# An encoder layer's gate-up groups: the last products and the first split reordered, and one queue of shared weight buffers

## The chip, the cores and the metric

The kernel runs on one core of one Trainium2 chip. The core has a matrix engine (TensorE, PE in the profile; its weight loads are PEld), a vector engine (VectorE, DVE), a scalar engine (ScalarE, ACT), GpSimd (POOL) and a synchronisation engine (SyncE, SP), which here issues most of the transfers from device memory. Each engine takes its instructions in order, and waits for others by semaphores. PE writes its sums into PSUM, eight banks of 128 x 512 float32. The metric is the device time of one execution in microseconds (us).

## The reference

One layer of an encoder, for 256 tokens of width 2048, in float32:

```python
x = x + 0.5 * post1(SwiGLU_1(pre1(x)))
h = pre_m(x); p = h @ W_in              # gated recurrence and windowed attention
x = x + post_m(concat(y_h, y_a) @ W_out)
x = x + 0.5 * post2(SwiGLU_2(pre2(x)))

def swiglu(x, w_gate_up, w_down):       # 2048 -> 2 x 5632 -> 2048
    gate, up = jnp.split(x @ w_gate_up, 2, axis=-1)
    return (jax.nn.silu(gate) * up) @ w_down
```

The change concerns `x @ w_gate_up` in the two feed-forward layers (FFN). All norms here divide by the root mean square.

## The kernel before

**Numbers in two parts.** PE multiplies in a format with fewer bits than float32. So each operand is split into a high part `h` (cast by ACT, line 176) and a low part `l` (the rest, subtracted by DVE, line 177), and each product is three products on PE: h with h, h with l, l with h (`three`, which issues them at line 441). A split of half a weight buffer, `split_half`, is one cast and one subtraction of 128 x 1024. The `h` and `l` buffers are five each, and one comes free when PE has made the last product that reads it.

**Groups and pairs.** The gate-up projection is made in 11 groups (`NG`) of 512 gate and the 512 matching up columns. A group has a 2 x 2 block of results in four PSUM banks, `c[m][n]`: m is the half of the tokens, n is gate or up. `c[0][0]` is called upper left, `c[0][1]` upper right, `c[1][0]` lower left, `c[1][1]` lower right. The sum runs over the width in eight pairs `u` of 128-row blocks. One pair needs 1 MB of weights, `raw`, with the blocks b11, b12 (first 128 rows; gate, up) and b21, b22, loaded by two transfers of 512 KB (line 152).

A plain pair makes eight block products, so 24 products on PE. A *mixed* pair (u = 2, 4, 5, 6; in group 1 only 2 and 4; none in group 0) makes seven block products, 21 on PE, after Strassen's scheme in a variant. For it, sums of weight blocks are formed in `raw`: `prepare` splits b11 (the `h1` and `l1` buffers) and then lets a GpSimd transfer add b12's and b22's source onto the first half of the buffer (line 901); `splits` does two additions on DVE (lines 915 and 916) and splits three halves, "lower", "upper" and "last". Four of the seven products go to four more PSUM banks, p1, p5, p6 and p7; the other three go to `c` directly. `products` (line 485) has their order: p1, upper left, upper right, p5, p7, p6, lower left.

**The boundary.** At the end of a group `boundary` (line 1101) brings the p banks home: ACT copies p1 (line 1112), DVE adds it to the upper left bank (1113), forms p1 + p6 (1116) and adds p7 (1117), adds this to the lower left bank (1118), and so on for upper right (1121, 1122) and lower right (1124, 1125). Pair 7 is plain and its 24 products come last, bank by bank: upper left and lower left after line 1118, upper right after 1122, lower right after 1125. Between 1113 and 1116 it asks for the first half of the split of the next group's pair 0; the second half comes at its end. Then `units` makes silu (ACT, 1039), the gated product (DVE, 1044), a transpose on PE (1064), and the split result `ht` for the down projection. In groups 2 to 5, two of the early `ht` tiles, 512 KB each, are stored to device memory by SP (`put_away`, line 1027), just after the split of pair 6 has been asked for.

**Order.** From group 1 on the order of every engine is written out (`manual_schedule`, line 1167). One function follows another as listed in `first_pairs`, `pair_ahead` and `boundary`: a pair's splits are asked for while the products of the pair before are still to come. Outside of that region a planner orders the instructions by its own estimates, so what is written last is not always last.

**Weight buffers.** Plain pairs use two buffers of the pool `gated.room`, mixed pairs three of `rawp`. `plan` loads the first five: (1,0) plain, (1,2) mixed, (1,1) plain, (1,4) mixed and (2,2) mixed, written (group, pair). After that each split, when it is done with a buffer, calls `load_next` for the next pair of the same kind. So in a usual group the split of pair 0 is followed by the load of pair 3, that of 1 by 7, that of 2 by 6, and those of 3, 4, 5, 6 and 7 by pairs 0, 2, 4, 5 and 1 of the next group. A load waits on SP until its buffer's last reader is done, and SP takes them in the order written.

Of the kernel before, what the change touches and what calls it, by code (L numbers as in the profile page):

```python
# [11 lines left out]
F32 = mybir.dt.float32  # L12
# [8 lines left out]
P = 128  # L21
# [3 lines left out]
KT = D // P  # L25
# [12 lines left out]
def hymba_layer_kernel(  # L38
# [25 lines left out]
    nc = tc.nc  # L64
# [3 lines left out]
    rawp = ctx.enter_context(tc.tile_pool(name="rawp", bufs=3))  # L68
# [7 lines left out]
    def nm(s):  # L76
        uid[0] += 1
        return f"{s}_{uid[0]}"

    def pa():  # L80
        return psum.tile([P, 512], F32, tag="pa", name=nm("pa"))

    def pb():
        return psum.tile([P, 512], F32, tag="pb", name=nm("pb"))
# [56 lines left out]
    def load(src, between=None, pool=rawp, **kw):  # L141
        raw = pool.tile([P, 2048], F32, tag="raw", name=nm("raw"), **kw)
        if len(src.shape) == 4:

            dst = raw.rearrange("p (a n b) -> p a n b", a=src.shape[1], n=src.shape[2])
            parts = [(dst[:, a], src[:, a]) for a in range(src.shape[1])]
        else:
            parts = [(raw.rearrange("p (a b) -> p a b", a=src.shape[1]), src)]
        for i, (to, of) in enumerate(parts):
            if i and between:  # L150
                between()
            nc.sync.dma_start(to, of)
        return raw
# [61 lines left out]
    last = {}  # L215
# [20 lines left out]
    def take(*a):  # L236
        take_hi(*a)
        take_lo(*a)
# [163 lines left out]
    class Blocks:  # L402
# [4 lines left out]
        ahead = None  # L407
# [74 lines left out]
            last = split_half(raw, 1)  # L482
            self.products(u, first, lower, upper, last)

        def products(self, u, first, lower, upper, last):

            if not self.p:
                self.p = [pa(), pa(), pb(), pb()]
            a, w = self.tiles[u], self.left_sums(u)

            def lhs(k, m):
                return [a[:, k, i, m * P : (m + 1) * P] for i in range(2)]

            def summed(j):
                return [w[:, j, i, :] for i in range(2)]

            def rhs(two, n):
                return [x[:, n * 512 : (n + 1) * 512] for x in two]

            for at, left, right in (  # L500
                (("p", 0), lhs(0, 0), first),
                (("c", 0, 0), lhs(1, 0), rhs(lower, 0)),
                (("c", 0, 1), summed(S4), rhs(lower, 1)),
                (("p", 1), summed(S1), rhs(upper, 0)),
                (("p", 3), summed(S3), rhs(upper, 1)),
                (("p", 2), summed(S2), rhs(last, 1)),
                (("c", 1, 0), lhs(1, 1), rhs(last, 0)),
            ):
                self.three(at, *left, *right)

        def fold(self):
# [331 lines left out]
    NG = DFF // 512  # L843
    NU = DFF // 256
    LATE = 8

    MIXED_IN = (2, 4, 5, 6)
    AWAY = 8
    MIXED = range(0, 20, 2)
    MIXED_EARLY = MIXED[:8]  # L850
# [4 lines left out]
    class Gated(Blocks):  # L855
# [20 lines left out]
        def plan(self):  # L876

            self.here = {g: MIXED_IN if g > 1 else MIXED_IN[:2] for g in range(1, NG)}
            self.kinds = {True: [], False: []}
            for g in range(1, NG):  # L880
                for u in range(KT // 2):
                    self.kinds[u in self.here[g]].append((g, u))
            self.raws, self.firsts, self.split_of = {}, {}, {}
            for mixed in (False, True, False, True, True):
                self.load_next(mixed)

        def load_next(self, mixed):

            if self.kinds[mixed]:
                g, u = self.kinds[mixed].pop(0)  # L890
                kw = {} if mixed else {"pool": self.room, "bufs": 2}
                self.raws[g, u] = load(self.source(u, g), **kw)

        def prepare(self, g, u):

# [12 lines left out]
        def splits(self, g, u):  # L908

            raw = self.raws[g, u]  # L910
            got = self.split_of[g, u] = []
            if (g, u) in self.firsts:
                b11, b12, b21, b22 = (raw[:, i * 512 : (i + 1) * 512] for i in range(4))
                got.append(split_half(raw, 1))
                nc.vector.tensor_tensor(b22, b11, b22, ALU.add)
                nc.vector.tensor_tensor(b21, b22, b21, ALU.add)
                yield
                got.append(split_half(raw, 0))
                yield
                got.append(split_half(raw, 1))  # L920
                self.load_next(True)
            else:
                got.append(split_half(raw, 0))
                yield
                got.append(split_half(raw, 1))
                self.load_next(False)
            yield

        def take(self, g, u):

            got = self.split_of.pop((g, u))
            del self.raws[g, u]
            first = self.firsts.pop((g, u), None)
            if first:
                self.products(u, first, *got)
                return ()
            hs, ls = zip(*got)
            return [
                (lambda k=k, m=m, n=n: self.plain(u, hs, ls, m, n, k))
                for k in range(2)  # L940
                for m in range(2)
                for n in range(2)
            ]
# [27 lines left out]
    def ffn(gated, w_dn, post_gain, again, gain=None, lead=None, aside=None):  # L971

        with ExitStack() as st:
            work = st.enter_context(tc.tile_pool(name=nm("wk"), bufs=1, reuse_waits="tile"))
            late = st.enter_context(tc.tile_pool(name=nm("hl"), bufs=LATE, reuse_waits="tile"))
            early_cm = tc.tile_pool(name=nm("he"), bufs=NU - LATE - AWAY, reuse_waits="tile")
            early = early_cm.__enter__()
# [5 lines left out]
            def room_for(tag):  # L983
                return work.tile([P, 512], F32, tag=tag, name=nm(tag))
# [28 lines left out]
            def sums_in(u):  # L1013
# [3 lines left out]
                ws = sums_of(whole, room_for("s").rearrange("p (j t) -> p j t", j=4))  # L1017
                apart = u == MIXED_IN[1]
                w = (gated.room if apart else work).tile(
# [13 lines left out]
            def units(c, scale):  # L1033
# [34 lines left out]
                for bank in banks:  # L1068
                    g = len(hts)
                    u = bank.rearrange("p (k t) -> p k t", k=2)  # L1070
                    if g in MIXED_EARLY:
                        u = room_for("z").rearrange("p (k t) -> p k t", k=2)
                        nc.scalar.copy(u.rearrange("p k t -> p (k t)"), bank)
                    pool = early if AWAY <= g < NU - LATE else late
                    ht = pool.tile([P, 2, 2, T], F32R, tag="ht", name=nm("ht"))
# [6 lines left out]
            def some(steps, n):  # L1082
                for _ in range(n):
                    next(steps)

            pre_stats()
            last = KT // 2 - 1
            for u in range(gated.pos, KT // 2):
# [4 lines left out]
                for done in {4: (0, 1, 2), 5: (3, 4), 6: (5, 6), 7: (7,)}.get(u, ()):  # L1093
                    even(done)
                    if done in MIXED_IN[:2]:
                        sums_in(done)
# [4 lines left out]
            def boundary(g):  # L1101

                a, b = room_for("z"), room_for("s")
                c, (p1, p5, p6, p7) = gated.c, gated.p
                add = nc.vector.tensor_tensor
                rest_of = gated.take(g, last)

                def bank(m, n):
                    for k in range(2):
                        rest_of[4 * k + 2 * m + n]()  # L1110

                nc.scalar.copy(a, p1)
                add(c[0][0], c[0][0], a, ALU.add)  # L1113
                ahead = gated.splits(g + 1, 0)
                next(ahead)
                add(b, p6, a, ALU.add)  # L1116
                add(a, p7, b, ALU.add)  # L1117
                add(c[1][0], c[1][0], a, ALU.add)  # L1118
                bank(0, 0)
                bank(1, 0)  # L1120
                add(b, p5, b, ALU.subtract)
                add(c[0][1], c[0][1], b, ALU.add)
                bank(0, 1)
                add(b, p5, a, ALU.subtract)
                add(c[1][1], c[1][1], b, ALU.add)
                bank(1, 1)
                next(ahead)

            def first_pairs(g, waiting):

                gated.group(g)
                some(waiting, 1)
                gated.prepare(g, MIXED_IN[1])
                some(waiting, 1)
                ahead = gated.splits(g, 1)
                some(ahead, 2)
                gated.prepare(g, MIXED_IN[2])
                for one in gated.take(g, 0):
# [9 lines left out]
            def pair_ahead(g, u):  # L1148

                ahead = gated.splits(g, u + 1)  # L1150
                next(ahead)
                if u + 1 == MIXED_IN[1]:
                    gated.prepare(g, MIXED_IN[3])
# [5 lines left out]
                if g == 1 and u in (4, 5):  # L1159
                    sums_in(MIXED_IN[u - 2])  # L1160
                if u == 5 and 1 < g <= AWAY // 2 + 1:
                    put_away(2 * g - 4)
# [4 lines left out]
            with tc.manual_schedule():  # L1167
                gated.prepare(1, MIXED_IN[0])
                some(gated.splits(1, 0), 2)
                for g in range(1, NG):  # L1170
# [3 lines left out]
                    if g < NG - 1:  # L1174
                        ahead = gated.splits(g, last)
# [24 lines left out]
            close_far()  # L1200
            back_cm = tc.tile_pool(name=nm("hb"), bufs=AWAY, reuse_waits="tile")
            back = back_cm.__enter__()
# [30 lines left out]
    gated = Gated(w_ffn1_gate_up[0], two_banks())  # L1233
    xt = new_xt()
    gated.see(xt)
    with tc.manual_schedule():
# [9 lines left out]
        raw = rawp.tile([P, 2048], F32, tag="raw", name=nm("raw"))  # L1246
        first = gated.source(0)
# [120 lines left out]
    with ExitStack() as s2:  # L1368
# [367 lines left out]
        for hp in range(4):  # L1736
            zf = headpair(2048 + hp * 256, "zf")
            if hp == 1:
                g = gates(0)
# [18 lines left out]
        g = gates(1)  # L1758
# [13 lines left out]
        gated = Gated(w_ffn2_gate_up[0], two_banks())  # L1772
# [80 lines left out]
```

## Time and profile before

| | |
|---|---|
| median of 3 runs | 1850.8 us (1848.57 to 1854.73) |
| the profiled execution | 1851.23 us, span 1849.5 us |
| PE busy | 1816.7 us, 98% |
| DVE busy | 1628.2 us, 88% |
| ACT busy | 1127.2 us, 61% |
| granted clock of PE | 0.999 |

Times in rows count from the start of the span. A row of the timeline gives start, duration, engine, line, operation, output and input tiles, and in brackets how long the engine was idle before it and what released it. Rows of one kind that follow each other are merged (x5). A product's record on PE lasts longer than the distance to the next product, since products overlap. The stretch from 313.49 to 356.37 us is one usual group: 42.88 us. The first FFN's groups 1 to 10 lie between about 57 and 490 us, the second's between about 1181 and 1610 us.

### The profile page before, as it was taken

Reading aid. Unit: us, or ns where it says so; the run is one execution under the profiler, and the core shown is the slowest. Engines: PE = TensorE matmul, PEld = TensorE weight load, DVE = VectorE, ACT = ScalarE, POOL = GpSimd, SP = SyncE. Lnnn points to the kernel's source line nnn. Section 1 sums busy time; section 2 is a strip of 40 time slices with the busy share of each in tenths; the row PEclk is TensorE's granted clock in tenths of the full one; section 3 lists DMA queues with packets and bytes.
Section 4 is the critical chain, followed back from the end, with each engine's and each line's share of the span. In section 5 each row is a group of like instructions: output and inputs, shape, how many; then the busy total and the mean of one; then the engine's idle time right before and its main releaser. Section 6 shows DMA issues by size and latency. Waiting matters only on the chain.

```text
span 1849.5 us, 23264 instructions
## 1 busy us (share of the span) xinstructions
PE 1816.7 (98%) x8438; PEld 1504.2 (81%) x8438; DVE 1628.2 (88%) x2071; ACT 1127.2 (61%) x1492; POOL 114.3 (6%) x115
## 2 busy tenths in 40 slices
PE   9999999999999999999999999999999999999998
PEld 7877878888887888888888888878888778888886
DVE  7999999998999999477687788899999999999897
ACT  7565556655665557477587556555666556666563
POOL 1011111111000000000000000011111111000000
PEclk9999999999999999999999999999999999999999
DMA  8789999888756566656554456789999888865565
GB/s 298 228 219 275 274 268 256 247 244 251 272 186 226 196 248 211 208 175 181 166 171 148 169 212 245 220 237 262 272 272 254 255 246 237 262 236 206 183 237 183
DMA packets 200020, 422.42 MB, mean 228 GB/s; under 512 B 10984, under 2 KB 45888, under 8 KB 199136
## 3 DMA queue, kind: packets, MB, share of 16 engines
q1 hardware_dynamic: 178880, 380.95, 59.9%
q0 software_dynamic: 21024, 39.99, 12.9%
q8 instruction: 66, 1.08, 0.2%
q14 instruction: 50, 0.41, 0.1%
HBM read 408.29 MB, written 12.60 MB: 228 GB/s over the span
## 4 chain that ended last, share of the span: by engine, by line
PE 70%; DVE 14%; DMA 8%; ACT 4%; issue 3%; SPq 1%; POOL 0%; DVEq 0%; ACTq 0%; POOLq 0%
PE pa L441 28%; PE pb L441 25%; DVE l L177 8%; DMA raw<-in_w_ffn_gate_up_dram 6%; PE pa L309 5%; PE pa L314 3%; ACT h L176 3%; PE pa L364 2%; PE pa L363 2%; PE pa L362 2%; DMA raw<-in_w_ffn_down_dram 2%; DVE pb L1118 1%; DVE z L1117 1%; DVE pa L1113 1%; DVE s L1116 1%
## 5 line engine op out<-in xcount | busy, mean ns | idle before, releaser
L176 ACT CAST h<-raw 128x1024 fp32r<-128x1024 f32 (+1 forms) x861 | 846.7, 1013 | 454.2 <-PE pb L441 113.2
L177 DVE TENSOR_TENSOR l<-raw,h 128x1024 fp32r<-128x1024 f32 (+1 forms) x861 | 985.0, 1170 | 136.8 <-ACT h L176 105.5
L441 PE MATMUL pa<-h,xt 128*128 128x512 f32 x1104 | 387.5, 392 | 0.2
L441 PE MATMUL pb<-h,xt 128*128 128x512 f32 x952 | 341.1, 393 | 17.5 <-DVE pb L1118 17.5
L441 PEld LDWEIGHTS pa<-h,xt 128*128 128x128 f32 x1104 | 207.4, 188 | 44.3 <-DVE xt L232 0.6
L441 PEld LDWEIGHTS pb<-h,xt 128*128 128x128 f32 x952 | 178.6, 188 | 64.4 <-DVE pb L1118 25.1
L441 PE MATMUL pa<-l,xt 128*128 128x512 f32 x552 | 215.7, 391 | 0.0
L441 PE MATMUL pb<-l,xt 128*128 128x512 f32 x476 | 185.5, 390 | 0.0
L441 PE MATMUL pb<-h,ht 128*128 128x512 f32 x464 | 163.5, 390 | 0.0
L441 PE MATMUL pa<-h,ht 128*128 128x512 f32 x464 | 162.7, 389 | 0.0
L901 POOL DMA_DIRECT2D raw<-in_w_ffn_gate_up_dram x76 | 92.0, 1211 | 758.1 <-DVE l L177 709.1
L309 PE MATMUL pa<-xt,h 128*128 128x512 f32 x512 | 124.4, 392 | 0.2 <-ACT h L176 0.2
L441 PEld LDWEIGHTS pa<-l,xt 128*128 128x128 f32 x552 | 103.9, 188 | 20.6 <-DVE l L177 0.7
L309 PEld LDWEIGHTS pa<-xt,h 128*128 128x128 f32 x512 | 93.8, 188 | 18.6 <-ACT h L176 0.6
L441 PE MATMUL pa<-h,xs 128*128 128x512 f32 x304 | 105.9, 389 | 0.0
L441 PE MATMUL pb<-h,xs 128*128 128x512 f32 x304 | 105.9, 389 | 0.0
L441 PEld LDWEIGHTS pb<-l,xt 128*128 128x128 f32 x476 | 89.4, 188 | 17.1
L441 PEld LDWEIGHTS pa<-h,ht 128*128 128x128 f32 x464 | 87.1, 188 | 18.2
L441 PEld LDWEIGHTS pb<-h,ht 128*128 128x128 f32 x464 | 87.1, 188 | 18.1
L441 PE MATMUL pb<-l,ht 128*128 128x512 f32 x232 | 90.3, 389 | 0.0
L441 PE MATMUL pa<-l,ht 128*128 128x512 f32 x232 | 90.3, 389 | 0.0
L314 PE MATMUL pa<-xt,l 128*128 128x256 f32 x512 | 69.1, 285 | 0.0
(289 smaller groups left out, 2517.6 us busy)
## 6 DMA issues: line engine op xcount, KB each, us to landing
raw<-in_w_ffn_gate_up_dram SPq DMA_DIRECT2D x350, 512.0 KB, 5.3
raw<-in_w_ffn_down_dram SPq DMA_DIRECT2D x88, 1024.0 KB, 5.2
raw<-in_w_mix_in_dram SPq DMA_DIRECT2D x52, 1024.0 KB, 5.0
raw<-in_w_ffn_gate_up_dram POOLq DMA_DIRECT2D x76, 512.0 KB, 8.3
raw<-in_w_mix_out_dram SPq DMA_DIRECT2D x16, 1024.0 KB, 5.0
away<-ht SPq DMA_DIRECT2D x16, 512.0 KB, 6.6
ht<-away SPq DMA_DIRECT2D x16, 512.0 KB, 7.4
pg<-in_post_norm_ffn_dram SPq DMA_DIRECT2D x4, 512.0 KB, 6.8
```

The source lines that it names most:

```text
L176: nc.scalar.copy(hi, src)
L177: nc.vector.tensor_tensor(lo, src, hi.bitcast(F32), ALU.subtract)
L309: nc.tensor.matmul(slot[f], weights(hs, kk, f), xcol(xt, k), start=(k == 0), stop=(k == KT - 1))
L314: nc.tensor.matmul(slot[f][:, 0:T], weights(ls, kk, f), xcol(xt, kh * 8 + kk, 0), start=False, stop=False,)
L362: nc.tensor.matmul(dst, xh, h[:, o : o + n], start=(k == 0), stop=False)
L363: nc.tensor.matmul(dst, xh, l[:, o : o + n], start=False, stop=False)
L364: nc.tensor.matmul(dst, xl, h[:, o : o + n], start=False, stop=(k == KT - 1))
L441: nc.tensor.matmul(self.bank(at), lhs, rhs, start=(n == 1), stop=n in (ends, self.of[at]), skip_group_check=n > ends,)
L901: nc.gpsimd.dma_start(raw[:, 0:1024].rearrange("p (k c) -> p k c", k=2), self.source(u, g)[:, :, 1], accum_op=ALU.add,)
L1113: add(c[0][0], c[0][0], a, ALU.add)
L1116: add(b, p6, a, ALU.add)
L1117: add(a, p7, b, ALU.add)
```

## The change

Three things are changed, all in the gate-up stage of both FFNs.

- In the last mixed pair (6) of groups 2 to 9 the upper right product comes last. The order is p1, upper left, p5, p7, p6, lower left, upper right. (Group 1 has pair 6 plain; group 10 keeps the old order.)
- In `boundary` the split of the next group's pair 0 is asked for whole, behind all additions and products.
- The five raw buffers are made once and shared by both kinds. Each split that is done with its buffer loads the next pair of one list into it. The list is sorted by when a pair is needed, where a mixed pair counts from its `prepare` (`PREPARED`): in a usual group 2, 0, 4, 1, 5, 3, 6, 7. So the split of pair 0 is followed by the load of pair 3, that of 1 by 6, that of 2 by 7, and those of 3, 4, 5, 6 and 7 by pairs 2, 0, 4, 1 and 5 of the next group. The first five loads are (1,2), (1,0), (1,4) into `rawp` and (1,1), (1,3) into the room.

```diff
-        def products(self, u, first, lower, upper, last):
+        def products(self, u, first, lower, upper, last, order=range(7)):
...
-            for at, left, right in (
+            seven = (
                 (("p", 0), lhs(0, 0), first),
                 (("c", 0, 0), lhs(1, 0), rhs(lower, 0)),
                 (("c", 0, 1), summed(S4), rhs(lower, 1)),
...
-            ):
+            )
+            for i in order:
+                at, left, right = seven[i]
                 self.three(at, *left, *right)
...
+    PREPARED = {2: -0.5, 4: 0.5, 5: 1.5, 6: 3.5}
...
-            self.kinds = {True: [], False: []}
+            wanted = []
             for g in range(1, NG):
                 for u in range(KT // 2):
-                    self.kinds[u in self.here[g]].append((g, u))
+                    before = PREPARED[u] if u in self.here[g] else u
+                    wanted.append((g * KT // 2 + before, g, u))
+            self.wanted = [at[1:] for at in sorted(wanted)]
             self.raws, self.firsts, self.split_of = {}, {}, {}
-            for mixed in (False, True, False, True, True):
-                self.load_next(mixed)
+            for pool, n in ((rawp, 3), (self.room, 2)):
+                for _ in range(n):
+                    raw = pool.tile([P, 2048], F32, tag="raw", name=nm("raw"), bufs=n)
+                    self.load_next(raw)
 
-        def load_next(self, mixed):
+        def load_next(self, raw):
 
-            if self.kinds[mixed]:
-                g, u = self.kinds[mixed].pop(0)
-                kw = {} if mixed else {"pool": self.room, "bufs": 2}
-                self.raws[g, u] = load(self.source(u, g), **kw)
+            if self.wanted:
+                g, u = self.wanted.pop(0)
+                dst = raw.rearrange("p (k n c) -> p k n c", k=2, n=2)
+                for k in range(2):
+                    nc.sync.dma_start(dst[:, k], self.source(u, g)[:, k])
+                self.raws[g, u] = raw
...
-                self.load_next(True)
+                self.load_next(raw)
...
-                self.load_next(False)
+                self.load_next(raw)
...
-                self.products(u, first, *got)
+                before_fold = g < NG - 1 and u == KT // 2 - 2
+                self.products(u, first, *got, (0, 1, 3, 4, 5, 6, 2) if before_fold else range(7))
...
                 add(c[0][0], c[0][0], a, ALU.add)
-                ahead = gated.splits(g + 1, 0)
-                next(ahead)
                 add(b, p6, a, ALU.add)
...
                 bank(1, 1)
-                next(ahead)
+                some(gated.splits(g + 1, 0), 2)
```

## The prediction

> **What bounds the kernel now.** I read the page's first part, the waits of TensorE, the timeline of PE, DVE and ACT around one group boundary, the windows of whole groups, and last the transfers.
>
> ```profile
> span 1849.5 us, 23264 instructions
> PE 1816.7 (98%) x8438; PEld 1504.2 (81%) x8438; DVE 1628.2 (88%) x2071; ACT 1127.2 (61%) x1492; POOL 114.3 (6%) x115
> ...
> PE pb L441 <- DVE pb L1118: 17.5, 18, 1.6
> PE pb L441 <- DVE l L177: 1.5, 2, 0.8
> PE pa L1064 <- DVE s L1044: 0.9, 1, 0.9
> ```
>
> The first line says that PE is the bound nearly everywhere; the list names what its gaps wait for (us, times, longest). Its one large wait is for L1118, the addition into the lower left bank, once at each of the 18 boundaries between gate-up groups (nine in each FFN). How long such a wait is, the starts of the products tell:
>
> ```profile
> 354.93 0.39 PE L441 MATMUL pa<-l,xt 128*128 128x512 f32 x1
> 355.16 0.39 PE L441 MATMUL pa<-h,xt 128*128 128x512 f32 x1
> 356.37 0.50 PE L441 MATMUL pb<-h,xt 128*128 128x512 f32 x1 [0.82 <-DVE pb L1118]
> 356.70 0.40 PE L441 MATMUL pb<-l,xt 128*128 128x512 f32 x1
> ...
> 360.65 0.39 PE L441 MATMUL pa<-h,xt 128*128 128x512 f32 x1
> ...
> 372.60 2.72 PE pa L441 x12
> ```
>
> Undisturbed, twelve products take 2.72, 0.227 each. After 355.16 the next was due at 355.39 and came at 356.37: 0.98 lost, where the idle column says 0.82, because a record lasts 0.39 and hides 0.16. The next group's first product stands at 360.65; from 355.39 it is 18 products away (banks lower left, upper right, lower right), so undisturbed it would come at 355.39 + 18 x 0.227 = 359.47. A usual boundary loses 1.18 in all: 0.98 in the wait and 0.2 in restarts. Over 18 boundaries: 17.5 + 18 x 0.16 = 20.4 of waits, and 18 x 0.2 = 3.6, together 24.0 us that could go. [...]
>
> ```profile
> 347.07 5.38 DVE L177 TENSOR_TENSOR l<-raw,h 128x1024 fp32r<-128x1024 f32 x5
> 352.37 0.69 DVE L1113 TENSOR_TENSOR pa<-pa,z 128x512 f32<-128x512 f32 x1
> 352.97 1.21 DVE L177 TENSOR_TENSOR l<-raw,h 128x1024 fp32r<-128x1024 f32 x1
> 354.10 0.68 DVE L1116 TENSOR_TENSOR s<-pb,z 128x512 f32<-128x512 f32 x1
> 354.82 0.69 DVE L1117 TENSOR_TENSOR z<-pb,s 128x512 f32<-128x512 f32 x1
> 355.61 0.70 DVE L1118 TENSOR_TENSOR pb<-pb,z 128x512 f32<-128x512 f32 x1
> 356.22 0.68 DVE L1121 TENSOR_TENSOR s<-pa,s 128x512 f32<-128x512 f32 x1
> 356.94 0.70 DVE L1122 TENSOR_TENSOR pa<-pa,s 128x512 f32<-128x512 f32 x1
> 357.67 0.69 DVE L1124 TENSOR_TENSOR s<-pa,z 128x512 f32<-128x512 f32 x1
> 358.39 0.70 DVE L1125 TENSOR_TENSOR pb<-pb,s 128x512 f32<-128x512 f32 x1
> 359.00 1.22 DVE L177 TENSOR_TENSOR l<-raw,h 128x1024 fp32r<-128x1024 f32 x1
> 360.13 0.74 DVE L1044 SCALAR_TENSOR_TENSOR z<-pa,scales,z 128x512 f32<-128x512 f32 x1
> ...
> 349.51 1.58 ACT L176 CAST h<-raw 128x1024 fp32r<-128x1024 f32 x2 [0.24 <-ACT h L176]
> 350.99 0.57 ACT L1112 COPY z<-pa 128x512 f32<-128x512 f32 x1
> 351.55 1.05 ACT L176 CAST h<-raw 128x1024 fp32r<-128x1024 f32 x1
> 358.45 0.69 ACT L1039 ACTIVATE z<-pa,scales 128x512 f32<-128x512 f32 x1 [4.54 <-DVE s L1124]
> ```
>
> The first twelve rows are DVE's, the last four ACT's. DVE runs without a gap, and its order is written out: whatever stands ahead of L1118 delays it. Between the first addition (352.37) and L1116 stands the split of the next group's first half (352.97), 1.13 of DVE on the path of L1118.
>
> **The change, part by part.**
>
> *The split goes behind the additions.* I move the rows up, keeping their own distances (0.60 after L1113, then 0.72, 0.79, 0.61, 0.72, 0.73, 0.72): L1116 352.97, L1117 353.69, L1118 354.48 to 355.18, L1122 355.81 to 356.51, L1125 357.26 to 357.96. From L1118's end to PE is 0.06 (356.31 to 356.37). PE wants the lower left bank at 355.39, the upper right at 356.75, the lower right at 358.11; the sums are there at 355.24, 356.57 and 358.02. The wait goes, with margins of 0.15, 0.18 and 0.09.
>
> The two halves of the split follow at 357.87 and 359.00, ending 359.09 and 360.22; L1044 starts at 360.13 as now. The next group's first `l` is wanted at 359.47 + 0.23 = 359.70, the second half's 12 products after 359.47, at 362.2: covers of 0.6 and 2. On ACT, silu waits for L1124, which is over 1.1 earlier.
>
> *The upper right product last.* The group's last mixed pair ends where the six products of the upper left bank begin, at 355.16 - 5 x 0.227 = 354.03; its 21 products began at 349.26. L1116 reads p6. In the old order p6 is products 16 to 18: the last starts at 353.12 and ends at 353.5, too late for 352.97. In the new one it is 13 to 15, ends at 352.8, and fits by 0.15. The upper right bank ends at 354.2, read by L1122 at 355.81: free. So the two edits need each other; with the split alone moved, L1116 would start near 353.6 and PE would still wait 0.4; with the order alone changed, the upper right bank and its buffer come later for nothing. The price: the buffer of the lower half is released at 354.2 instead of 351.5, and ACT's first cast for the next group moves from 351.55 to 354.3; with the second it is done by 356.4, wanted at 357.87.
>
> *Group 1.* Its pair 6 isn't mixed, so only the split moves.
>
> ```profile
> 93.66 0.69 DVE L1113 TENSOR_TENSOR pa<-pa,z 128x512 f32<-128x512 f32 x1
> ...
> 97.66 0.50 PE L441 MATMUL pb<-h,xt 128*128 128x512 f32 x1 [1.34 <-DVE pb L1118]
> ```
>
> L1118 would end 2.81 after L1113's start, at 96.47, PE could go at 96.53, and wants to at 96.17 (97.66 less 1.34 idle and 0.16): 0.36 and 0.2 of restart stay, twice.
>
> *Five shared buffers, in order of need.* The same transfers in the same two pieces of 512 KB, no more instructions on SP or POOL. What triggers them differs: plain pair 1 of the next group now follows the split of pair 6 (was 7); pair 6 that of pair 1 (was 2); mixed pair 5 that of pair 7 (was 6). These matter where `ht` is put away, groups 2 to 5:
>
> ```profile
> 133.81 2.05 SPq L152 DMA_DIRECT2D raw<-in_w_ffn_gate_up_dram  x2
> 135.91 1.07 SPq L1027 DMA_DIRECT2D away<-ht  x2
> 137.08 2.54 SPq L152 DMA_DIRECT2D raw<-in_w_ffn_gate_up_dram  x2
> ...
> 147.72 1.05 ACT L176 CAST h<-raw 128x1024 fp32r<-128x1024 f32 x1 [3.12 <-DMA raw<-in_w_ffn_gate_up_dram]
> 163.80 4.42 ACT L176 CAST h<-raw 128x512 fp32r<-128x512 f32 x5 [3.91 <-DMA raw<-in_w_ffn_gate_up_dram]
> ...
> core 0: us, PE busy (x) PEld busy (x) DVE busy (x) ACT busy (x) POOL busy (x), PEclk, DMA share, GB/s
> ...
> 356.37:399.26 42.89, 42.07 (x188) 34.45 (x189) 39.90 (x48) 26.07 (x30) 4.84 (x4) 1.00 0.87 244
> ...
> 140.58:184.58 44.00, 42.32 (x188) 34.37 (x188) 39.79 (x48) 25.24 (x30) 4.85 (x4) 1.00 0.92 273
> ```
>
> Pair 1's load, issued at 137.08 behind the writes, lands 10.6 later and holds ACT for 3.12; pair 6's holds it for 3.91; that group then takes 44.00. Now pair 1 goes ahead of the writes and pair 6 a pair sooner. Pair 5 takes the place behind the writes, and at 147.7 it is just in time: its first cast follows pair 1's two. The extra waits of such groups are inside the 20.4 above.
>
> *Start of the stage.* The first loads change too: a buffer freed late now takes pair 4 of group 1, where it took one of group 2.
>
> ```profile
> 1176.29 1.20 SPq L152 DMA_DIRECT2D raw<-in_w_ffn_gate_up_dram  x2
> ...
> 54.99 0.62 ACT L176 CAST h<-raw 128x512 fp32r<-128x512 f32 x1 [4.19 <-DMA raw<-in_w_ffn_gate_up_dram]
> ...
> 1180.61 2.01 ACT L176 CAST h<-raw 128x1024 fp32r<-128x1024 f32 x2 [3.23 <-issue]
> ```
>
> Landing 4.1 to 5.3 later (5.3 is the page's median for these), at 1180.4 to 1181.6, its cast (0.53) pushes those at 1180.61, and the silu behind them, by 0.3 to 1.5; PE waits for that silu's product already (L1064, 0.9). The planner, which orders this part, may do better or worse: -0.5 to 2; I take 0.9, the middle. In the first FFN ACT waits for such a load even now, until 54.99, and the list of PE's waits has nothing from it: I take 0.2 of 0 to 1.
>
> At the end of the stage the three buffers that the down projection takes over were last used by pairs 4, 5 and 6 of group 10, and are now by 3, 4 and 5. They come free earlier, and PE waits for no load there: zero.
>
> *The sum.* 24.0, less 0.1 at each of 16 usual boundaries (the margins of 0.09 to 0.18 are thin; bounds 0 and 0.25), 1.6; less 2 x 0.55 for group 1; less 1.1 at the starts: 20.2 gained. The profiled execution took 1851.23 (span 1849.5 and 1.7 around it), 0.4 over the median of 1850.8. From the median: **1830.6**.
>
> **The rivals.**
>
> *Transfers become the bound where `ht` is put away.* For: a DMA share of 0.92 at 273 GB/s in 140.58 to 184.58. Against: 0.92 x 44.00 is 40.5, under the 41.7 that a group would take. If these eight groups keep their period, 8 x 1.18 comes back: 1840. Chance 0.12.
>
> *The bubble stays: DVE can't follow.* PE gains 1.18 a group, DVE has the same work; its casts wait for `h` buffers (0.24 at 349.51). If DVE's slack is spent, L1113 slips after PE by as much, and the wait returns: about 1849. Against: DVE works 39.9 of 42.89 and L1113's start hangs on PE's own release at 349.26, so it comes earlier with PE. [...] Chance 0.05.
>
> *Slower: pair 5's load lands too late.* Behind the writes it heads ACT's queue before pair 2's casts, and all behind wait. In group 3 PE reaches pair 2's first use at about 156.1 (139.6 for the bank, 4.1, then two pairs of 5.44, transposes 0.8, and 0.7); casts and split need 2.8 before, so it may land 16 after its issue without harm. Each us beyond costs 8; 18.7 cancels the gain, at 19.5 it is 1857. Against: 10.6 now. Chance 0.07.
>
> *Thinner margins than read:* 0.4 left at each boundary, 1836 to 1838. Chance 0.08.
>
> **How the numbers follow.** Forecast 0.68, at 1826 to 1835 by its bounds: nothing left at any boundary and the start 0.5 better, against 0.25 left at each and 3 lost at the starts. Adding the thin margins and most of the transfer case gives 1826 to 1841 for eight in ten. A change of 0.3% (5.6 us) is about what a measurement tells from none. Faster: 0.68 + 0.12 + 0.08 = 0.88; same 0.05; slower 0.07.
>
> **What would show it.** L1118 gone from PE's waits except some 0.4 at the two group-1 boundaries; DVE's additions 0.6 to 0.8 apart without L177 among them; usual groups 41.7 to 41.8 long; ACT without its 3.12 and 3.91 waits in groups 2 to 5. Wrong, if a new wait on `l` or on a transfer stands at the boundaries, or a planned part outside them grows.

## The result, and the profile after

| | before | changed |
|---|---|---|
| median | 1852.8 us (1848.57 to 1855.65) | **1831.6 us** (1830.0 to 1832.88) |
| ratio, with its 95% interval | | **0.9887** (0.9864 to 0.991) |
| a second time | 1850.2 us | 1831.8 us, ratio 0.9902 (0.9887 to 0.9917) |
| span of the profiled execution | 1849.5 us | 1831.1 us, the second time 1829.1 us |

The page's first lines for the changed kernel, and rows of PE's waits (us in total, times, longest):

```profile
span 1831.1 us, 23305 instructions
...
PE 1814.2 (99%) x8438; PEld 1504.0 (82%) x8438; DVE 1627.3 (89%) x2071; ACT 1129.4 (62%) x1492; POOL 114.4 (6%) x115
...
PE pb L441 <- DVE l L177: 1.5, 2, 0.8
...
PE pb L441 <- ACT h L176: 1.3, 1, 1.3
PE pa L1074 <- DVE s L1054: 0.9, 1, 0.9
...
PE pb L441 <- DVE pb L1126: 0.4, 2, 0.2
```

The lower left addition (now L1126) has gone from 17.5 us in 18 waits to 0.4 in two, which are those of group 1. New is one wait of 1.3 for a cast; it is outside the groups, and is taken up below. The boundary that answers to the one shown of before, in the timeline (start, duration, engine, line; PE, then DVE, then ACT):

```profile
345.77 0.39 PE L441 MATMUL pa<-h,xs 128*128 128x512 f32 x1
...
347.13 0.39 PE L441 MATMUL pa<-h,xt 128*128 128x512 f32 x1
347.36 0.39 PE L441 MATMUL pb<-h,xt 128*128 128x512 f32 x1
...
351.55 0.39 PE L441 MATMUL pa<-h,xt 128*128 128x512 f32 x1
...
356.99 0.27 PE L1074 MATMUL pa<-ident,z 128*128 128x128 f32 x1
...
344.34 0.69 DVE L1123 TENSOR_TENSOR pa<-pa,z 128x512 f32<-128x512 f32 x1
344.94 0.68 DVE L1124 TENSOR_TENSOR s<-pb,z 128x512 f32<-128x512 f32 x1
345.65 0.69 DVE L1125 TENSOR_TENSOR z<-pb,s 128x512 f32<-128x512 f32 x1
346.45 0.70 DVE L1126 TENSOR_TENSOR pb<-pb,z 128x512 f32<-128x512 f32 x1
347.06 0.68 DVE L1129 TENSOR_TENSOR s<-pa,s 128x512 f32<-128x512 f32 x1
347.84 0.70 DVE L1130 TENSOR_TENSOR pa<-pa,s 128x512 f32<-128x512 f32 x1
348.58 0.69 DVE L1132 TENSOR_TENSOR s<-pa,z 128x512 f32<-128x512 f32 x1
349.30 0.70 DVE L1133 TENSOR_TENSOR pb<-pb,s 128x512 f32<-128x512 f32 x1
349.91 2.35 DVE L177 TENSOR_TENSOR l<-raw,h 128x1024 fp32r<-128x1024 f32 x2
...
344.16 1.05 ACT L176 CAST h<-raw 128x1024 fp32r<-128x1024 f32 x1 [0.62 <-PE pb L441]
345.52 1.06 ACT L176 CAST h<-raw 128x1024 fp32r<-128x1024 f32 x1 [0.30 <-PE pb L441]
```

PE goes from the last product of the upper left bank (347.13) to the first of the lower left (347.36) in 0.23, without a wait: L1126 ended at 347.15. The next group's first product stands at 351.55. The split (L177, 2.35 for both halves) stands behind the last addition. Two windows of the changed kernel (length, then busy time with instructions of PE, PEld, DVE, ACT and POOL, granted clock, DMA share, GB/s), over three of the four groups of a stage where `ht` is put away, and over a usual group:

```profile
core 0: us, PE busy (x) PEld busy (x) DVE busy (x) ACT busy (x) POOL busy (x), PEclk, DMA share, GB/s
104.50:230.00 125.50, 125.50 (x567) 103.53 (x565) 119.58 (x143) 77.92 (x90) 14.72 (x13) 1.00 0.93 275
...
356.99:398.79 41.80, 41.80 (x189) 34.48 (x188) 39.83 (x49) 26.08 (x30) 4.84 (x4) 1.00 0.90 252
```

PE is busy in all of both. By the starts of PE's rows (the transposes after each group, the middle part's first product at line 309, the last product) the execution divides so, in us:

| stretch | before | changed | changed, second time |
|---|---|---|---|
| start to group 0's transposes | 62.6 | 62.5 | 63.3 |
| groups 1 to 10 of the first FFN | 433.0 | 421.8 | 421.8 |
| its down projection and what follows, to line 309 | 291.5 | 293.8 | 290.9 |
| middle part, to the second FFN's group 0 | 399.4 | 399.9 | 400.3 |
| groups 1 to 10 of the second FFN | 433.4 | 423.3 | 423.3 |
| its down projection | 220.5 | 220.9 | 220.6 |

The gain is in the groups: 11.2 and 10.1, together 21.3. Usual groups went from 42.87 to 41.80.

### The profile page after: what moved, and what is told of

Its sections match the earlier page's. It is cut to its first block, busy times and chain, and to the rows that moved or that the text cites. A ratio compares the mean times of both kernels' runs of the same rounds, so it can differ in the third digit from the quotient of the medians.

```text
span 1831.1 us, 23305 instructions
## 1 busy us (share of the span) xinstructions
PE 1814.2 (99%) x8438; PEld 1504.0 (82%) x8438; DVE 1627.3 (89%) x2071; ACT 1129.4 (62%) x1492; POOL 114.4 (6%) x115
## 4 chain that ended last, share of the span: by engine, by line
PE 87%; DVE 5%; ACT 3%; DMA 3%; issue 2%; POOL 0%; SPq 0%; DVEq 0%; ACTq 0%; POOLq 0%
PE pa L441 37%; PE pb L441 33%; PE pa L309 5%; DVE l L177 3%; PE pa L314 3%; DMA raw<-in_w_ffn_gate_up_dram 2%; PE pa L364 2%; PE pa L362 2%; PE pa L363 2%; ACT h L176 1%; PE pa L1074 1%; PE pb L1074 1%; PE pb L1582 0%; PE pb L1556 0%; PE pb L1660 0%
## 5 line engine op out<-in xcount | busy, mean ns | idle before, releaser
L177 DVE TENSOR_TENSOR l<-raw,h 128x1024 fp32r<-128x1024 f32 (+1 forms) x861 | 983.1, 1171 | 118.3 <-ACT h L176 83.8
L441 PEld LDWEIGHTS pb<-h,xt 128*128 128x128 f32 x952 | 178.6, 188 | 43.2 <-DVE pb L1133 3.5
L441 PEld LDWEIGHTS pa<-h,ht 128*128 128x128 f32 x464 | 87.7, 189 | 18.4
```

Of the source, the lines that this page charges most:

```text
L177: nc.vector.tensor_tensor(lo, src, hi.bitcast(F32), ALU.subtract)
L441: nc.tensor.matmul(self.bank(at), lhs, rhs, start=(n == 1), stop=n in (ends, self.of[at]), skip_group_check=n > ends,)
```

## The experiments

My theory: DVE's order at the boundary (the order of its instructions) made the wait; both edits there are needed to end it; the shared buffers keep late loads out of the groups with put-away transfers. The rivals: one edit does it all, the loads do it, or DVE as a whole is the bound. Ratios are to the kernel before, run beside each; a "period" is the time from one group's transposes to the next's.

### The split alone

```diff
                 add(c[0][0], c[0][0], a, ALU.add)
-                ahead = gated.splits(g + 1, 0)
-                next(ahead)
                 add(b, p6, a, ALU.add)
...
-                next(ahead)
+                some(gated.splits(g + 1, 0), 2)
```

> The kernel before, with the next group's first half of a split moved behind all result additions; order of products and buffers as before. My theory (the wait is made by the work that stands ahead of the lower left addition on DVE, and the upper right product in its old place gives out p6 too late): 0.4 of the wait and 0.2 of restart stay at each of the 18 boundaries where 0.98 and 0.2 stood, so usual groups take 42.3 us instead of 42.87, PE's list still has the lower left addition with some 18 waits, and the whole is about 10 us faster (ratio near 0.9946). Rival, the split's place is all that counts: groups 41.8, 20 us faster. Rival, DVE or the transfers set the period: groups stay at 42.9 and the time as before.

Measured: ratio 0.9946 (0.9932 to 0.9959), usual periods 42.32. PE's wait for the lower left addition (here L1116) and the DVE row that makes it:

```profile
PE pb L441 <- DVE pb L1116: 5.7, 18, 0.5
...
349.75 0.69 DVE L1114 TENSOR_TENSOR s<-pb,z 128x512 f32<-128x512 f32 x1 [0.48 <-PE pb L441]
```

DVE stands 0.48 for p6, as the theory has it. The groups take 11.2 us less, so half of the gain needs only this edit.

### The order of products alone

```diff
-                self.products(u, first, *got)
+                before_fold = g < NG - 1 and u == KT // 2 - 2
+                self.products(u, first, *got, (0, 1, 3, 4, 5, 6, 2) if before_fold else range(7))
```

> The kernel before, with the upper right product of the last mixed pair made last; the half split stays between the first and the second addition, buffers as before. My theory: the lower half's buffer is released 2.7 later, so ACT's first cast for the next group starts at about its old place plus 2.7 and the half split on DVE, and every addition behind it, stands some 2.4 later: PE waits 3.4 for the lower left addition in place of 0.98, usual groups take 45.3 us, and the whole is about 39 us slower at 16 boundaries (ratio near 1.021). Rival, the order alone is the gain, since it gives out p6 sooner: faster by up to 20. Rival, the order does nothing by itself: groups 42.9, the time as before.

Measured: ratio 1.0027 (1.0015 to 1.0038), usual periods 43.25 and not 45.3. The sign is right, the size is off by a factor of eight. Rows of ACT and DVE at a boundary:

```profile
353.19 1.06 ACT L176 CAST h<-raw 128x1024 fp32r<-128x1024 f32 x1 [0.62 <-PE pb L441]
...
353.37 0.69 DVE L1116 TENSOR_TENSOR pa<-pa,z 128x512 f32<-128x512 f32 x1
354.27 1.22 DVE L177 TENSOR_TENSOR l<-raw,h 128x1024 fp32r<-128x1024 f32 x1 [0.21 <-ACT h L176]
```

The cast did not wait for the lower half's buffer, which the last product reads, but went ahead of the first addition: it got the buffer whose last reader comes first in the new order, that of the upper half. (What ended its wait is a product into `pb`, as p7, the upper half's last reader, is; the upper right product writes `pa`.) So the half split slipped by 0.3 and not by 2.4. My step was wrong in which buffer is handed out.

### Both edits at the boundary, old buffers

The two diffs above together, with the loads of the kernel before.

> Both edits at the boundary (split behind the additions, upper right product last) with the raw buffers and the order of loads of the kernel before. My theory: the usual groups without put-away transfers (the last four before the end of each stage) take 41.8 us as in the changed kernel, and only groups 2 to 5 of each stage, where ht is put away, keep late loads (ACT's waits of 3 to 4 us for raw), which cost 0.3 to 1.2 each now: 3 to 8 us in all, so 1835 to 1840, ratio 0.991 to 0.994. Rival, the order of the loads carries the gain: groups stay near 42.9 everywhere and the time as before. Rival, the shared buffers do nothing: all groups 41.8 and the time of the changed kernel, ratio 0.9887.

Measured: ratio 0.993 (0.9917 to 0.9942). The groups after the put-aways take 41.8; eight periods around them take 42.5 to 43.2, 8.2 us above 41.8 in sum. The waits of PE, and two of ACT's:

```profile
PE pb L441 <- DVE pb L1119: 4.0, 10, 0.5
...
146.06 1.05 ACT L176 CAST h<-raw 128x1024 fp32r<-128x1024 f32 x1 [3.81 <-DMA raw<-in_w_ffn_gate_up_dram]
161.51 4.42 ACT L176 CAST h<-raw 128x512 fp32r<-128x512 f32 x5 [3.94 <-DMA raw<-in_w_ffn_gate_up_dram]
```

The late loads come back as waits for the addition, since the casts and splits that they delay stand ahead of it on ACT and DVE: after the cast at 161.51, DVE has no gap over 0.22 until that boundary's first addition at 178.28.

### The shared buffers alone

The diff of `plan` and `load_next` alone.

> The kernel before with the five raw buffers shared and loaded in order of need, and nothing else. My theory: the wait of 0.98 for the lower left addition stays at every boundary and usual groups stay at 42.9; only the three groups that a late load lengthened (by 1.16, 0.3 and 0.55 over 42.87) lose their extra: 2 us faster, ratio 0.999, not to be told from no change. Rival, loads in order of need are a gain of their own: usual groups under 42.5, 6 us faster or more.

Measured: ratio 1.0001 (0.9993 to 1.001); all usual periods 42.87, the longer ones among them gone (2.0 us less in the groups). The wait for the addition stays:

```profile
PE pb L441 <- DVE pb L1125: 15.8, 18, 1.3
```

So the buffers are worth nothing that the times can tell alone and 8 us beside the other two edits. I read from these sums that most of a late load's delay hid in the wait of 0.98 that stood there anyway; no row shows it by itself.

### Loads by number

```diff
-    PREPARED = {2: -0.5, 4: 0.5, 5: 1.5, 6: 3.5}
+    PREPARED = {2: 2, 4: 4, 5: 5, 6: 6}
```

> The changed kernel with its five shared buffers loaded in the order of the pairs' numbers (0 to 7) and not in order of need. If the order of need carries what the shared buffers give (8 us beside the edits at the boundary, by the run with the old buffers): the mixed pairs 4 and 5, which are cast early in a group, have their loads issued only when pair 7 of the group before and pair 0 are split, some 4 us before they are wanted with 5.3 to land; ACT then stands 1 to 3 us for raw in every group, groups take 42.0 to 43.0, and the whole 1835 to 1850 (ratio 0.992 to 0.999). If sharing alone carries it: groups 41.8, ratio 0.989.

Measured: ratio 0.9977 (0.9968 to 0.9986), so 14 us of the gain are lost, within the range that was expected, but elsewhere: only five periods around the put-aways are longer (42.0 to 43.1), the others take 41.8. The rest is lost at the start of the stages, 6.4 to 7.2 us at each, of which the second FFN's first period gives 1.4 back. (The profiled execution, 1849.7 us, is the longest of eleven with a median of 1845.9, so its parts add up to more than 14.)

```profile
60.33 0.49 PE L441 MATMUL pa<-h,xt 128*128 128x512 f32 x1 [2.97 <-ACT h L176]
...
1184.21 0.79 PE L441 MATMUL pa<-h,xt 128*128 128x512 f32 x1 [3.61 <-ACT h L176]
```

Pair 2 of group 1, prepared first, is now loaded third. After each of these waits PE's products stood 0.43 apart for a while (62.18 to 67.30 and 1186.06 to 1190.33), where they are 0.23 apart before and after; the execution's mean granted clock is 0.994, against 0.997 and 0.999 in the two of the changed kernel.

### The addition made twice

```diff
                 add(b, p6, a, ALU.add)
+                add(b, p6, a, ALU.add)
```

> The changed kernel with the addition of p6, the second of each boundary, made twice: 0.61 us more on DVE ahead of the lower left bank. If DVE's chain of additions is what sets PE's start there, with a margin of 0.15 by the prediction: a wait of 0.46 and 0.17 of restart at 16 boundaries and 0.6 at two, usual groups 42.4 instead of 41.8, 11 us slower than the changed kernel, ratio to before 0.995, and the lower left addition back in PE's list 18 times. If the margin is larger than read, groups stay nearer to 41.8; if DVE as a whole were the bound, 0.61 of work would cost 0.61 in every group with no wait at this place.

Measured: ratio 0.9976 (0.9966 to 0.9987), 13.6 us more in the groups than in the changed kernel, usual periods 42.55. One boundary:

```profile
350.03 0.68 DVE L1124 TENSOR_TENSOR s<-pb,z 128x512 f32<-128x512 f32 x1
350.75 0.69 DVE L1125 TENSOR_TENSOR s<-pb,z 128x512 f32<-128x512 f32 x1
...
353.02 0.50 PE L441 MATMUL pb<-h,xt 128*128 128x512 f32 x1 [0.41 <-DVE pb L1127]
```

The repeat costs 0.72, not 0.61. PE comes at 353.02 where 352.46 was due: 0.56 = 0.72 less 0.16, so the margin of 0.15 was read rightly. With the restart a period is 0.75 longer, about as much as DVE's added work, so this run alone does not rule out DVE as a whole; the two that leave DVE's work as it is and change its order (the split alone, and half the split ahead of the upper right bank) do.

### The addition made five times

The same with four additional lines.

> The changed kernel with that addition made five times. By the same theory the wait is four times 0.61 less 0.15, 2.3 us, with 0.2 of restart: usual groups 44.3, 45 us slower than the changed kernel, ratio to before 1.013. It also gives 18 waits of 2.3 us with PE at work on both sides: if a single wait of that length is enough for a stretch at half clock, each is followed by 3.4 us at 0.5, which costs 1.7 more (groups 46, ratio near 1.03); if not, the clock stays at 1.0 in all groups.

Measured: ratio 1.0313 (1.0295 to 1.0331). Six periods take 44.7, which is three times 0.72 over 42.55. The other twelve take 1.3 to 1.8 more than this kind of wait explains, one of them 2.8: the usual ones among them 46.0 to 46.6 and 47.5. Windows around one boundary of the second kind, each 3.41 long, columns as above:

```profile
363.83:367.24 3.41, 3.41 (x17) 2.83 (x16) 3.38 (x5) 2.48 (x4) 1.22 (x1) 1.00 0.94 319
367.24:370.65 3.41, 1.27 (x6) 0.73 (x4) 3.17 (x6) 0.32 (x1) 0.00 (x0) 1.00 0.94 251
370.66:374.07 3.41, 2.98 (x7) 2.40 (x8) 3.24 (x6) 0.71 (x2) 0.00 (x0) 0.50 0.71 132
374.07:377.49 3.42, 3.42 (x16) 2.78 (x16) 3.42 (x5) 3.35 (x5) 0.00 (x0) 1.00 0.27 48
```

PE is busy in the first window, stands for most of the second, has half the clock for all of the third, and the whole of it again in the fourth. My two cases were each half right: after some of these waits the clock stood at 0.5 for a stretch, as here, and after others it did not: a period of 44.69 (200.60 to 245.29) has a mean of 1.00.

### The same work at two places

```diff
                 add(b, p6, a, ALU.add)
+                add(b, p6, a, ALU.add)
+                add(b, p6, a, ALU.add)
...
                 add(b, p5, a, ALU.subtract)
+                add(b, p5, a, ALU.subtract)
+                add(b, p5, a, ALU.subtract)
```

> As much repeated DVE work at each boundary as with the addition made five times, but at two places: the addition of p6 three times (2 x 0.72 more ahead of the lower left bank) and the last subtraction three times (2 x 0.72 more ahead of the lower right bank). By the chain of additions: two waits of about 1.3, groups 44.7 as with five times. [...] Two waits of 1.3 with 2.7 of products between put at most some 1.7 into any one stretch: no half clock at any boundary, and 18 x 2.9 = 52 us over the changed kernel, ratio 1.018 where five times gave 1.031. Rival, it is the waiting as such, however spread, that halves the clock: as many stretches at 0.5 as there (13 in the groups), ratio near 1.031.

Measured: ratio 1.0178 (1.0161 to 1.0195); all usual periods 44.71 to 44.75, and the granted clock 1.00 from 201.10 to 245.83 and from 319.00 to 361.00, and 0.999 over the execution, where five additions had 0.987:

```profile
PE pb L441 <- DVE pb L1137: 22.7, 18, 1.3
PE pb L441 <- DVE pb L1128: 21.6, 18, 1.7
```

The 2.9 us a period are there as with five additions, but parted in two they cost some 24 us less in all: between these two kernels, what the clock added went with how the waiting was spread. That waits so spread, some 1.7 to a stretch, would leave the clock whole was my estimate; the clock was 0.999 here, and no run shows where a bound lies.

### Half the split ahead of the upper right bank

```diff
                 bank(0, 0)
                 bank(1, 0)
+                ahead = gated.splits(g + 1, 0)
+                next(ahead)
                 add(b, p5, b, ALU.subtract)
...
-                some(gated.splits(g + 1, 0), 2)
+                next(ahead)
```

> The changed kernel with the next group's first half split (1.13 us of DVE) between the lower left addition and the additions of the upper right bank. If DVE's order decides at each bank by itself, the upper right sum comes 1.13 later against a margin of 0.18: 0.95 of wait and 0.2 of restart, now at the first product of the upper right bank, at every boundary; usual groups 42.95, 21 us slower than the changed kernel, ratio near 1.001, so the whole gain is gone although the lower left addition has no wait. If only the first bank's sum is critical, because six products stand ahead of the upper right bank: groups 41.8, ratio 0.990.

Measured: ratio 1.0004 (0.9995 to 1.0014), periods 42.95. PE's only large wait is now one bank later:

```profile
PE pa L441 <- DVE pa L1132: 15.0, 18, 0.9
```

Each bank's sum is on PE's path by itself. The whole gain is gone, though the 1.13 us of DVE stand behind the first bank's sum.

### The changed kernel again

> The changed kernel once more, for what its first trace showed outside the gate-up groups: in the first FFN's down projection PE stood for 1.27 and 0.77 us with one product between, and then ran 3.4 us at a granted clock of 0.5. If both come from the change itself, they are here again at the same place, and the part from the last group's transposes to the middle part's first product takes 293.8 us again, against 291.5 before. If the transfer's landing varies by itself (it landed 7.8 us after its issue there, 6.8 before), the first stall is shorter or gone, and with it the stretch at half clock, and the part takes 291 to 292. The groups take 41.8 either way, and the ratio is 0.989.

Measured: ratio 0.9902, the groups as in the first profile, 290.9 from the last transposes to line 309. The place in the first FFN's down projection, in the timeline of the first profile and then of the second:

```profile
559.51 0.49 PE L441 MATMUL pb<-h,sp 128*128 128x512 f32 x1 [1.27 <-ACT h L176]
560.77 0.50 PE L441 MATMUL pb<-l,sp 128*128 128x512 f32 x1 [0.77 <-DVE l L177]
...
562.37 0.63 PE L441 MATMUL pa<-h,ht 128*128 128x512 f32 x1
562.79 0.63 PE L441 MATMUL pa<-l,ht 128*128 128x512 f32 x1
```

```profile
560.12 0.50 PE L441 MATMUL pb<-l,sp 128*128 128x512 f32 x1 [0.76 <-DVE l L177]
```

The first wait was gone, and with it the products 0.42 apart. The 2.4 us that the down projection and what follows lost in the first profile belong to that execution, not to the change: in the twelve other profiles, of all kernels, this part took 289.9 to 292.1. Over all profiles the first wait is between 0 and 1.3; whether the shared buffers make it a little longer on average stays open.

### The late buffer last

```diff
-            for pool, n in ((rawp, 3), (self.room, 2)):
-                for _ in range(n):
-                    raw = pool.tile([P, 2048], F32, tag="raw", name=nm("raw"), bufs=n)
-                    self.load_next(raw)
+            for pool, n in ((rawp, 3), (rawp, 3), (self.room, 2), (self.room, 2), (rawp, 3)):
+                raw = pool.tile([P, 2048], F32, tag="raw", name=nm("raw"), bufs=n)
+                self.load_next(raw)
```

> The changed kernel with the five buffers handed out in another order at the start of each stage: the two early ones of the first pool, the two of the second, and the first pool's third, which comes free late, last (it then takes pair 3 and not pair 4 of group 1). With the shared buffers, the part from the middle's first product to the second FFN's first transposes took 399.9 to 400.3, with the old ones 399.4 to 399.5, and a wait of 0.5 for the first product of gate and up was new there in most runs. If the late load of pair 4 makes this, the part takes 399.5 and the wait is gone: 0.7 us here, perhaps 0.3 in the first FFN, ratio 0.9895 where the changed kernel has 0.990, not to be told apart by the times. If the planner's order makes it, 400 stays.

Measured: ratio 0.9888 (0.9873 to 0.9902), median 1829.5 us. The middle part takes 399.5, and this row of the changed kernel's second profile, at the second FFN's group 0, is absent:

```profile
PE pa L1074 <- DVE z L1054: 0.5, 1, 0.5
```

That row alone would prove little, since the changed kernel's first profile lacks it too. The part's time says more: it took 399.8 to 400.4 in all seven profiles with the buffers shared and loaded as in the change, the one with the shared buffers alone (400.1) among them, and 399.4 to 399.5 in the four with the old buffers. So the late load of pair 4 made the difference. The start of the first FFN, 62.95, did not move. The first FFN's down projection with what follows took 289.9, the shortest of all profiles, without a wait over 0.25 at the place shown above; the edit also changes which buffers the last pairs of a stage use, and whether that is the reason is not shown. By its median this is the fastest of the kernels, but it can't be told from the changed kernel by the times.

## Why the prediction was right

**The waits.** Forecast were 24.0 that could go, less 1.6 for thin margins and 1.1 for group 1: 21.3 in the groups. Measured were 21.3. Step by step: the additions came 0.60, 1.31, 2.11, 3.50 and 4.96 after the first, forecast 0.60, 1.32, 2.11, 3.44 and 4.89. L1126 ended at 347.15 with PE due to need it by 347.30: the margin is 0.15, as read. The 0.1 a boundary was right in size and came otherwise than I had it: not as a wait, but as 18 products that took 4.19 (347.36 to 351.55) where 4.08 is the undisturbed time. That the size agreed is luck, and why these products are slower is not shown. In group 1 PE lost 0.37 and 0.36 beside the restart, where 0.36 was forecast, for each FFN.

**The two edits need each other.** Right for the whole gain: alone they gave 0.9946 and 1.0027. The split with the shared buffers and the old order was not run; by the usual periods of the split alone, 42.32 against 41.80, the order is worth some 0.5 at each of 16 boundaries beside it, an estimate of 8 us. The step on the buffers of `h` was wrong. I had ACT's first cast at 1.93 after the first addition, waiting for the lower half's buffer; it started 0.18 before that addition (344.16 and 344.34). In the changed kernel nothing hangs on this, since the split's cover is there; for the order alone it made my expectation 39 us where 5 were measured.

**The shared buffers.** Right in the end state: between 106 and 235 us, ACT's longest wait for `raw` is 0.97, where 3.12 and 3.91 stood. Pair 5's load behind the writes landed in time, the rival's limit being 16 after its issue; rows of SP and ACT for group 3:

```profile
134.33 29.43 SPq L900 DMA_DIRECT2D raw<-in_w_ffn_gate_up_dram  x12
...
144.69 2.53 ACT L176 CAST h<-raw 128x512 fp32r<-128x512 f32 x3 [0.50 <-DMA raw<-in_w_ffn_gate_up_dram]
```

That is 10.4 after the first issue, and ACT waited 0.50. What I had not worked out is what the old loads would cost beside the faster boundary: I counted 2 us of theirs inside the waits of before, and with the old buffers it was 8.2. This did not touch the sum, because the changed kernel has no such loads left.

**The starts.** Forecast 0.9 lost in the second FFN and 0.2 in the first. Measured 0.4 and 0.8 in the second (399.9 and 400.3 against 399.4), by the late load that was named, as the late buffer put last shows; in the first nothing beyond what varies between executions.

**Down projection.** Forecast zero. One execution lost 2.4 and another gained 0.6; the first loss stands outside what the other twelve profiles show, so zero stands for the change; that an execution may lose some us there was not in my account.

**The sum.** 20.2 forecast, and 18.4 and 20.4 measured between the spans; the medians, 1831.6 and 1831.8, stand 1.0 and 1.2 over the forecast. Between medians taken side by side the gain was 21.2 and 18.4, so a distance of 1 us lies within the scatter of the times. Two figures beside the sum were added up wrongly: the low end of the range is 1827.4 by its two terms (1830.6 less 1.6 and 1.6), not 1826, and the landing that cancels the gain comes 18.5 after the issue (20.2 at 8 for each us), not 18.7. Neither bears on the forecast.

**The rivals:** the put-away groups take 41.80 like the others at a DMA share of 0.93, so transfers are not the bound there. DVE as a whole is not either: half the split moved ahead of the upper right bank adds no work to DVE, and the whole gain is gone, with the wait at that bank. Nor did a lack of buffers make most of the wait: with the split alone moved, and every buffer as it was, the wait went from 17.5 to 5.7.

## What to carry to other kernels

When an engine waits at the same place in every round, list in order what stands ahead of the releasing instruction on its engine. Move behind it the work whose result is wanted late, and reckon with the spacing that the rows show; then find the next instruction that was hidden by the wait. An edit that does nothing alone can be worth much beside another, since a wait can hide a delay that is shorter than it: try edits together before one is dropped. If an order of products is changed, look up anew which buffer comes free first.

## What the runs showed of the hardware that I had not expected

The granted clock fell to 0.5 after some waits of PE and not after others. In the changed kernel's first profile PE was busy for 1.38 of the 3.42 us from 558.20 to 561.62, with the waits of 1.27 and 0.77 and a product between them; the clock was 1.00 there, 0.50 from 561.62 to 565.03, and 1.00 from there to 568.45. Products stood 0.43 apart at 0.50 and 0.23 at 1.00. In the second profile, with the wait of 0.76 alone, PE was busy for 2.65 of the 3.41 us from 558.93 to 562.34, and its products behind the wait stood 0.23 apart.

With five additions, PE's busy time leaves 2.58 in each of two periods: the one from 200.60 to 245.29 took 44.69 at a mean granted clock of 1.00, the one from 336.18 to 382.16 took 45.98 at 0.96, with the 3.41 at 0.50 shown above in it: 1.29 more for the same waiting. With the same work at two places, PE's busy time leaves 2.41 of the period from 201.10 to 245.83, with the clock at 1.00. So the waiting of a whole period did not tell whether the clock fell; what decides it is not shown.

In the kernel with the addition made twice, the repeat, which writes the tile just written, started 0.72 after the first (350.03 and 350.75). The first addition's follower, which reads nothing that the first one wrote and writes another tile, started 0.60 after it (349.43 and 350.03).
